# State space tables and phases on VectorE, parameters of both layers at once, and finer pieces stepped by VectorE's load

## The chip, the cores and the metric

The kernel runs on one core of a Trainium2 chip. Its engines work side by side, each from a queue of its own, and wait for one another by semaphores: TensorE (PE, with its weight loads PEld), VectorE (DVE), ScalarE (ACT), GpSimd (POOL) and SyncE (SP), which here issues DMAs. The metric is the time of one execution on the device in microseconds (us), as the median of the runs.

## What is computed

Two layers of a backbone over 1024 latent tokens and 256 context tokens of width 1024, in float32. In each layer a normed and modulated input is projected once, and three groups of heads share the columns: six latent attention heads, a bidirectional state space part (S5) of 16 groups with 16 channels and 64 states, and six windowed attention heads. Their outputs are joined, projected and added; then a gated MLP with a small convolution follows. Cut to what matters here:

```python
def s5_discretize(a_re, a_im, log_dt, b_re, b_im):
    lam = lax.complex(a_re, a_im)
    dt = jnp.exp(log_dt)[:, None]
    a_bar = jnp.exp(lam * dt)
    b_bar = ((a_bar - 1.0) / lam)[:, :, None] * b_mat
...
for l in range(DEPTH):
    cq, ckv, kr, u, qs, ks, vs = jnp.split(h @ w_in[l], IN_OFFSETS, axis=-1)
    ya = mla_latent_attention(...)     # six heads, softmax over all tokens
    yb = s5_bidirectional(u, ...)      # h[t] = a_bar h[t-1] + b_bar u[t], both directions, y = Re(C h) + D u
    yc = swa_latent_attention(...)     # windowed heads
    x = x + g1 * (jnp.concatenate([ya, yb, yc], axis=-1) @ w_out[l])
    x = x + g2 * conv_ffn(rms_norm(x, norm2[l]) * (1.0 + sc2) + sh2, ...)
```

## The kernel before

Each layer runs through an input projection, an attention stage, an output projection and the MLP. The change is in the attention stage, from about 296 to 723 us in layer 0 and from 2107 to 2500 us in layer 1.

**The latent heads** set the stage's pace. A unit is one head and one chunk of tokens (512, 512 or 256). `mla_prep` makes it ready: it transposes kn and qn on PE, splits them into a rounded part (kh, qh, by ACT) and a rest (kl, ql, by DVE, line 98), and then takes the maximum of the scores: twelve products b<-kh,qh on PE, each followed by a `tensor_reduce` to mx on DVE (line 1336), then nm (line 1340), which a transposition, ACT and a DMA carry into a row of qh. `mla_steps` then runs the unit's ten steps (two for the short chunk): three products into s on PE, an exponential to p on ACT, one product av on PE. The preparation of the next unit is drawn in between the steps of this one.

**S5** runs as a side job in the same stage. It is a Python generator, `s5()`; wherever it yields, a piece ends. `side.share(done, nsteps * 5 // 6)` after each attention step draws as many pieces as bring it level with its share, in layer 0 all pieces by step 110 of 132. `S5N` gives the number of pieces, 161 and 138. The work goes by quarters of four groups, with the 128 partitions holding two directions of 64 states, and time cut into 160 windows of eight tokens:
- parameters: from a_re, a_im and log_dt, by some 170 DVE instructions on 16 to 64 columns, the powers pw of a_bar, the decay rho, the factor of bb, and a ladder ec, ei of squarings of the rotation of one step;
- `windows`: the channels transposed into windows, with copies cpx and cpl on DVE (lines 1049, 1050);
- `tables(k)`: output map cv and input map q of quarter k, complex products of pc or pq (powers in window order) with C or bb; six products of 128x640 and six of 128x512, all on GpSimd;
- `phases(k)`: the rotations E of 160 windows, by doubling from one column, eight levels of six products each, all on GpSimd;
- `maps(k)`: q transposed to wl, and cv x bb multiplied on PE to the map inside a window (strip, Mt); `inputs(k)`: ug x wl on PE; `recur(k)`: rotate by E, scan with rho (line 1156), rotate back to Sg, on DVE; `outputs(k)`: Mt x ug and cv x Sg on PE; `back`: channels back to rows.

A third job, `mods`, sums later layers' modulation vectors on DVE (macc<-mw,srow,macc, line 98), drawn in the same way. PE's matmuls of preparation, S5 and mods share three PSUM banks b; the scores s have three of their own.

The order in which each engine gets its instructions is not the program's order: a list scheduler places them, so that work of several jobs is mixed. Each engine then runs its own list strictly in order. Loads go through SP's queue in the same fixed way. All the helpers `mul`, `add` and `sub` record line 80, `ts` lines 93 and 95, `stt` line 98, `act` line 77, `mm` line 65 and `tr` line 74, so rows are told apart by their tiles. In the changed kernel all DVE instructions carry line 50.

Of the kernel before, what the change touches and what calls it, by code (L numbers as in the profile page):

```python
# [8 lines left out]
F32 = mybir.dt.float32  # L9
F32R = mybir.dt.float32r  # L10
I32 = mybir.dt.int32
# [21 lines left out]
def trunk(ctx, tc, x, c, ctxt, c_ctx, w_mod, b_mod, norm1, w_in, q_lora_g, w_uq, kv_lora_g, w_ukv,  # L33
# [4 lines left out]
    V, S, G, PE = nc.vector, nc.scalar, nc.gpsimd, nc.tensor  # L38
# [65 lines left out]
    def load_split(hi, lo, raw, srcs, scale=None):  # L104
        """DRAM pieces into raw, then hi = the rounded value and lo = what is left of it."""
        for dst, src in srcs:
            nc.sync.dma_start(out=dst, in_=src)
        if scale is None:
            act(hi, raw)
            sub(lo, raw, f32(hi))  # L110
        else:
            act(hi, raw, AF.Copy, scale=scale)
            stt(lo, raw, scale, f32(hi), ALU.mult, ALU.subtract)

    class Wsets:
        """Rotating sets of (rounded, rest, raw) weight tiles over the pools that are open."""
# [49 lines left out]

    def k8(t):
        return t.rearrange("p (k n) -> p k n", k=8)
# [72 lines left out]
    def mod_cols(psf, pl, acc, l, nm, k0, n, nj):  # L241
        """Sums over the partitions of acc, n blocks of 128 columns for each of nj."""
# [13 lines left out]
    def mod_gen(l, nm, nj, pl, psf, w):  # L256
        """One modulation vector, with the sums over the rows on the vector engine."""
# [15 lines left out]
    def norm_stats(big, sm, psf, xs, ci, rn, o=0, n=None, eng=None):  # L273
        """rn[p, i] = 1 / rms of token i * 128 + p of the chunk (or of n of its tokens from o)."""
# [22 lines left out]
    def norm_apply(tb, rbt, psf, rn, xs, at, A, sh, ci, o=0, n=None, eng=G):  # L297
        """at = x * rn * A + sh, split; tb and rbt are scratch."""
# [24 lines left out]
    def load_mov(cols, src, k0, m):  # L323
        """Columns of rows k0.. as a moving operand: m tiles of 128 rows in one set."""
# [27 lines left out]
    def s1_tiles(t0, m):  # L352
        """Tiles of tokens side by side, as the rows of the operands arrive."""
# [87 lines left out]
    def params(rows, name):  # L441
        """Vectors of both layers, rows of 128 values each, with the channel on the partitions."""
# [71 lines left out]

    for l in range(2):
# [6 lines left out]
        # ======== input projection ========  # L522
# [45 lines left out]
        def rope_table(g, half):  # L568
            """Cosines and sines of the latent tokens, times the gains of the dimensions they meet."""
# [9 lines left out]
        def rope(xv, tab, g, t, nh, half, eng=None):  # L579
            """Gain and rotation of [128, 2, nh, 2 half] in place, two tiles of tokens."""  # L580
# [35 lines left out]
        # k_rope, windowed keys and values, with the token on the partitions  # L616
# [51 lines left out]
        def s3(state):  # L668
            """Keys and values of the latent attention, from a chunk of c_kv."""
# [35 lines left out]
        def s5q(state):  # L705
            """Queries of the latent attention, from a chunk of c_q."""
# [25 lines left out]
        def s7(t0):  # L732
            """Queries of the windowed attention."""
# [108 lines left out]
        # ======== S5 ========  # L842
        def s5():
            sp = s5p
            cnt = [0]
# [10 lines left out]
            def s16(dt=F32, n=16):  # L856
                cnt[0] += 1
                return sp.tile([128, n], dt, name=f"s16_{cnt[0]}")

            prm = sp.tile([128, 3, 16], F32, name="prm")  # L860
            ld = sp.tile([16, 2], F32, name="ld")
            nc.sync.dma_start(out=ld, in_=log_dt[l].rearrange("d g -> g d"))
            ps = bank([128, 512])
            for i, src in enumerate((a_re, a_im, None)):
                st = sp.tile([16, 2, 64], F32, name=f"pst{i}")
                if src is None:
                    V.tensor_copy(st, ld.unsqueeze(2).to_broadcast([16, 2, 64]))
                else:
                    nc.sync.dma_start(out=st, in_=src[l].rearrange("d g p -> g d p"))
                tr(ps[:, i * 16:(i + 1) * 16], st.rearrange("g d p -> g (d p)"))  # L870
            V.tensor_copy(prm.rearrange("p a g -> p (a g)"), ps[:, 0:48])
            lre, lim = prm[:, 0, :], prm[:, 1, :]

            def expo(dst, xin):
                xc, k, r, q = s16(), s16(), s16(), s16()
                ki, kj = s16(I32), s16(I32)
                ts(xc, xin, -87.0, 88.0, ALU.max, ALU.min)
                ts(k, xc, 1.4426950408889634, MAGIC)
                ts(k, k, -MAGIC, op0=ALU.add)
                stt(r, k, -0.693359375, xc)  # L880
                stt(r, k, 2.12194440e-4, r)
                ts(q, r, 1.0 / 5040)
                for cf in (1.0 / 720, 1.0 / 120, 1.0 / 24, 1.0 / 6, 0.5, 1.0):
                    stt(q, q, cf, r, ALU.add, ALU.mult)
                ts(q, q, 1.0, op0=ALU.add)
                ts(ki, k, 127.0, op0=ALU.add)
                ts(kj, ki, 23, op0=ALU.logical_shift_left)
                mul(dst, q, kj.bitcast(F32))

            def sincos(co, si, a):  # L890
                k, r, z, p, s0, c0 = (s16() for _ in range(6))
                ki, k1 = s16(I32), s16(I32)
                m, sg, w = s16(), s16(), s16()
                ts(k, a, 0.6366197723675814, MAGIC)
                ts(k, k, -MAGIC, op0=ALU.add)
                stt(r, k, -1.5703125, a)
                stt(r, k, -4.837512969970703125e-4, r)
                stt(r, k, -7.549789948768648e-8, r)
                mul(z, r, r)
                ts(p, z, -2.5052108385441720e-8, 2.7557319223985893e-6)  # L900
                mul(p, p, z)
                for cf in (-1.9841269841269841e-4, 8.3333333333333333e-3, -1.6666666666666667e-1):
                    stt(p, p, cf, z, ALU.add, ALU.mult)
                mul(p, p, r)
                add(s0, p, r)
                ts(p, z, 2.0876756987868099e-9, -2.7557319223985888e-7)
                mul(p, p, z)
                for cf in (2.4801587301587302e-5, -1.3888888888888889e-3, 4.1666666666666667e-2, -0.5):
                    stt(p, p, cf, z, ALU.add, ALU.mult)
                ts(c0, p, 1.0, op0=ALU.add)  # L910
                V.tensor_copy(ki, k)
                ts(k1, ki, 1, op0=ALU.bitwise_and)
                V.tensor_copy(m, k1)
                ts(w, m, -1.0, 1.0)
                mul(r, s0, w)
                mul(z, c0, m)
                add(si, r, z)
                mul(r, c0, w)
                mul(z, s0, m)
                add(co, r, z)  # L920
# [46 lines left out]
            for _ in range(10):  # L967
                nr, ni = s16(), s16()
                if _ == 5:
                    yield  # L970
# [1106 lines left out]
```

## Time and profile before

| | us |
|---|---|
| median of three runs | 3424.99 |
| lowest, highest run | 3420.28, 3428.63 |
| the profiled execution's span | 3426.8 |
| PE busy in it | 3253.7 (95%) |
| DVE busy | 2339.9 (68%) |
| ACT busy | 1167.5 (34%) |
| POOL busy | 486.9 (14%) |

A row of a timeline tells when an instruction started and how long the profiler had it in its engine, with the time that the engine sat idle ahead of it and what released it in brackets. "Busy" thus includes time in which an instruction has started and makes no headway. Windows give the busy time of each engine in a stretch, and the TensorE clock that was granted, as a share of full speed (1.00 is 2.4 GHz, 0.50 is 1.2 GHz).

### The profile page before, as it was taken

The numbers are of one execution on the slowest core, as the hardware profiler recorded it, in microseconds if no ns is written. First come the engines' busy times: TensorE is split into PE (matmuls) and PEld (weight loads), VectorE is DVE, ScalarE is ACT, GpSimd is POOL, SyncE is SP. The second block draws the span as 40 slices with busy tenths as digits, with TensorE's granted clock in tenths as the row PEclk, the third lists the DMA queues.
The fourth block names the chain that finished last, engine by engine and source line by source line (L and its number), as shares of the span: only waits on it lengthen the run. The fifth ranks groups of instructions, "written<-read, shape, count | busy, mean of one in ns | idle before, by whom it ended". The sixth has DMA issues, their size and how long they took to land. (4 is left out here: it accounts for less than half of the span.)

```text
span 3426.8 us, 43150 instructions
## 1 busy us (share of the span) xinstructions
PE 3253.7 (95%) x15950; PEld 2597.1 (76%) x15950; DVE 2339.9 (68%) x4391; ACT 1167.5 (34%) x2076; POOL 486.9 (14%) x787
## 2 busy tenths in 40 slices
PE   8999769999999999999999999679999999999999
PEld 5897446667888888888888887446677788888888
DVE  7778786885687766667666768776762665555655
ACT  3532225555152222222223442234563422222221
POOL 2332561000020000000000432471000100000000
PEclk9999789999999999999999999789999999999999
DMA  7434111333512222222212344010324111111211
GB/s 247 132 87 125 32 50 41 98 116 100 166 47 77 64 73 73 64 65 78 62 59 68 101 117 116 18 31 23 87 71 124 44 44 49 56 43 43 62 37 56
DMA packets 401325, 260.84 MB, mean 76 GB/s; under 512 B 173647, under 2 KB 370393, under 8 KB 401113
## 3 DMA queue, kind: packets, MB, share of 16 engines
q1 hardware_dynamic: 400466, 257.80, 26.0%
q8 instruction: 126, 2.06, 0.2%
q14 instruction: 86, 0.70, 0.1%
q10 hardware_dynamic: 647, 0.26, 0.0%
HBM read 206.22 MB, written 49.46 MB: 75 GB/s over the span
## 5 line engine op out<-in xcount | busy, mean ns | idle before, releaser
L65 PE MATMUL u<-ah,wh 128*128 128x512 f32 (+1 forms) x1760 | 649.9, 370 | 2.3 <-ACT ah L77 1.6
L65 PE MATMUL u<-al,wh 128*128 128x512 f32 (+1 forms) x1760 | 648.9, 369 | 1.4 <-POOL al L80 1.1
L65 PE MATMUL u<-ah,wl 128*128 128x512 f32 (+1 forms) x1760 | 648.3, 368 | 0.0
L77 ACT ACTIVATE wh<-raw 128x1024 fp32r<-128x1024 f32 (+3 forms) x184 | 189.2, 1038 | 720.5 <-PE d L65 292.2
L98 DVE SCALAR_TENSOR_TENSOR cv<-u,par,cv 128x511 f32<-128x511 f32 (+2 forms) x616 | 326.1, 555 | 135.6 <-ACT cv L77 130.4
L65 PEld LDWEIGHTS u<-al,wh 128*128 128x128 f32 x1760 | 332.3, 189 | 58.2 <-POOL al L80 2.2
L65 PEld LDWEIGHTS u<-ah,wh 128*128 128x128 f32 x1760 | 332.0, 189 | 57.8 <-ACT ah L77 1.8
L65 PEld LDWEIGHTS u<-ah,wl 128*128 128x128 f32 x1760 | 332.2, 189 | 55.3
L80 DVE TENSOR_TENSOR wl<-raw,wh 128x1024 fp32r<-128x1024 f32 (+3 forms) x184 | 220.1, 1200 | 160.0 <-ACT wh L77 158.9
L98 DVE SCALAR_TENSOR_TENSOR x<-d,g,x 128x512 f32<-128x512 f32 (+2 forms) x307 | 209.5, 685 | 108.8 <-PE d L65 108.6
L98 DVE SCALAR_TENSOR_TENSOR macc<-mw,srow,macc 128x256 f32<-128x256 f32 (+1 forms) x364 | 231.3, 660 | 67.1 <-DMA mw<-in_w_mod_dram 65.8
L77 ACT ACTIVATE cv<-u,par,par 128x512 f32<-128x512 f32 (+1 forms) x220 | 159.7, 728 | 323.1 <-PE u L65 320.9
L65 PE MATMUL av<-p,v 128*65 128x512 f32 (+1 forms) x504 | 260.7, 601 | 0.0
L77 ACT ACTIVATE p<-s 128x512 f32<-128x512 f32 (+1 forms) x252 | 147.6, 586 | 236.4 <-PE s L65 233.1
L65 PE MATMUL d<-ah,wh 128*128 128x512 f32 (+2 forms) x614 | 224.8, 366 | 1.8 <-DVE x L98 1.6
L65 PE MATMUL d<-al,wh 128*128 128x512 f32 (+2 forms) x614 | 223.5, 364 | 0.0
L65 PE MATMUL d<-ah,wl 128*128 128x512 f32 (+2 forms) x614 | 223.4, 364 | 0.0
L1336 DVE TENSOR_REDUCE mx<-b 128x1 f32<-128x512 f32 (+1 forms) x300 | 165.6, 586 | 47.6 <-PE b L65 46.3
L65 PE MATMUL b<-kh,qh 96*128 96x512 f32 (+1 forms) x300 | 124.7, 462 | 63.0 <-DVE ql L98 46.0
L65 PE MATMUL s<-qh,kh 97*128 97x512 f32 (+1 forms) x252 | 154.0, 611 | 0.0
L65 PEld LDWEIGHTS b<-kh,qh 96*128 96x128 f32 x300 | 57.9, 199 | 114.5 <-DVE ql L98 50.8
L65 PE MATMUL av<-sp,sv 128*65 128x384 f32 x320 | 129.0, 492 | 6.5 <-ACT sden L77 3.4
(373 smaller groups left out, 6689.4 us busy)
## 6 DMA issues: line engine op xcount, KB each, us to landing
raw<-in_w_up_dram SPq DMA_DIRECT2D x88, 512.0 KB
mw<-in_w_mod_dram SPq DMA_DIRECT2D x224, 128.0 KB
raw<-in_w_down_dram SPq DMA_DIRECT2D x44, 512.0 KB
mw<-in_w_mod_dram SPq DMA_DIRECT2D x48, 256.0 KB
wm<-in_w_mod_dram SPq DMA_DIRECT2D x16, 512.0 KB
xd<-x SPq DMA_DIRECT2D x32, 256.0 KB
raw<-in_w_in_dram SPq DMA_DIRECT2D x14, 512.0 KB
sqd<-sqb SPq DMA_DIRECT2D x36, 192.0 KB
```

Source lines behind the costliest of these rows:

```text
L65: PE.matmul(out, lhsT, rhs, start=start, stop=stop)
L77: S.activation(out, in_, func, **kw)
L80: (eng or V).tensor_tensor(out, a, b, op=op)
L98: V.scalar_tensor_tensor(out, a, s, b, op0=op0, op1=op1)
L1336: V.tensor_reduce(mx[:, j, i:i + 1], ps[:, :w], axis=AX.X, op=ALU.max)
```

## The change

Five things are altered together.

1. `tables(k)` runs on VectorE, the input map q first and then cv; every product is followed by a yield. GpSimd keeps only the memsets of Sg in this stage.
2. `phases(k)` is no longer a doubling. E is one complex outer product of two small tables, EP (10 values, coarse) and EQ (16 values, fine): six products of 128x640 per quarter, on VectorE.
3. The parameters of both layers are worked out together, once, by `s5_params` in layer 0's stretch where the u features are projected, on tiles with a layer axis. They go to DRAM (pmd, 128x1168 values for each layer, 598 KB) and `s5()` reads its layer's part back into pm with one DMA. Layer 1 works out none.
4. The copies cpx, cpl, pc, pq and the negated nct move from VectorE to ScalarE.
5. The pieces are finer, and a piece weighs what it costs: `Metered` wraps VectorE and adds 100 plus the elements of each instruction to a load; `Weighed.to` advances by 200 plus the load that a piece recorded. `S5N` becomes 175700 and 166800. `phases(k)` moves behind `inputs(k)`, `tables(k + 1)` behind `recur(k)`.

```diff
-    V, S, G, PE = nc.vector, nc.scalar, nc.gpsimd, nc.tensor
+    S, G, PE = nc.scalar, nc.gpsimd, nc.tensor
+    class Metered:
...
+            def call(out, *args, **kw):
+                self.load += 100 + max(int(np.prod(a.shape[1:])) for a in (out, *args[:1]) if hasattr(a, "shape"))
+                return fn(out, *args, **kw)
+            return call
+    V = Metered(nc.vector)
...
-    S5N = [161, 138]
+    S5N = [175700, 166800]
...
+    class Weighed(Side):
+        def to(self, k):
+            while self.k < k and not self.done:
+                at = V.load
+                try:
+                    next(self.g)
+                except StopIteration:
+                    self.done = True
+                self.k += 200 + V.load - at
...
+    def s5_params(sp, psf):
...
+        for l in range(2):
+            ld = sp.tile([16, 2], F32, name=f"ld{l}")
+            nc.sync.dma_start(out=ld, in_=log_dt[l].rearrange("d g -> g d"))
...
+        V.tensor_copy(prm.rearrange("p a l g -> p (a l g)"), ps[:, 0:96])
+        yield
...
+        for E, lev, size in ((EQ, 3, 16), (EP, 7, 10)):
...
+                cmul(E[0][:, :, n:n + m, :], E[1][:, :, n:n + m, :], E[0][:, :, 0:m, :], E[1][:, :, 0:m, :], er, ei2, sh)
+                n *= 2
+                lev += 1
+                yield
+        for l in range(2):
+            nc.sync.dma_start(out=pmd[l], in_=J[:, l, :])
+        yield
...
+            pm = sp.tile([128, NPRM], F32, name="pm")
+            nc.sync.dma_start(out=pm, in_=pmd[l])
+            pw, rho, (fr, fi), EP, EQ = prm_views(pm)
...
-                V.tensor_copy(pc[i][0:64, 0:9, :], pw[i][0:64])
+                act(pc[i][0:64, 0:9, :], pw[i][0:64])
...
-            ts(nct, ct[1], -1.0)
+            act(nct, ct[1], AF.Copy, scale=-1.0)
...
-                        V.tensor_copy(cpx, unc[:, :, cs])
-                        V.tensor_copy(cpl, un[:, :, cs])
+                        act(cpx, unc[:, :, cs])
+                        act(cpl, un[:, :, cs])
...
-                mul(t1, pr, cr, G)
-                mul(t2, pi, ci_, G)
-                sub(cv[0], t1, t2, G)
+                mul(t1, pr, cr)
+                yield
+                mul(t2, pi, ci_)
+                yield
+                sub(cv[0], t1, t2)
+                yield
...
-                n, lev = 1, 3
-                while n < 160:
-                    m = min(n, 160 - n)
...
+                a = [z[:, :, gs].rearrange("p t g -> p g t").unsqueeze(3).to_broadcast(sh) for z in EP]
+                b = [z[:, :, gs].rearrange("p t g -> p g t").unsqueeze(2).to_broadcast(sh) for z in EQ]
+                Ev = [z.rearrange("p g (a b) -> p g a b", a=10) for z in E]
+                yield from cmul(Ev[0], Ev[1], a[0], a[1], b[0], b[1], sh, "pm")
...
-            tables(0)
+            yield from tables(0)
             yield from windows(0)
-            phases(0)
             for k in range(4):
                 yield from maps(k)
-                if k < 3:
-                    tables(k + 1)
                 if k == 2:
                     yield from windows(1)
                 yield from inputs(k)
+                yield from phases(k)
                 yield from recur(k)
                 if k < 3:
-                    phases(k + 1)
+                    yield from tables(k + 1)
                 yield from outputs(k)
...
-        side = Side(s5(), S5N[l])
+        side = Weighed(s5(), S5N[l])
+        if l == 0:
+            prm_pool, close_prm = open_pool("prm", side=sd)
+            prms = Side(s5_params(prm_pool, lambda: cps.tile([128, 512], F32, tag="b", name="b", bufs=3)), 30)
+            prms.to(1)
...
-                if f * 3 + ci == 2:
-                    side.to(6)
+                if l == 0:
+                    prms.share(f * 3 + ci + 1, 6)
         prep.finish()
+        if l == 0:
+            prms.finish()
+            close_prm()
+        side.to(1)
```

How it stands on three engines, all in layer 0. First GpSimd, where the phases of quarter 1 end and the tables of quarter 2 begin (E: phases; pm, cm: halves of complex products), before:

```order
L80 TENSOR_TENSOR E_4459<-cm_4533,cm_4534 128x4x32
L80 TENSOR_TENSOR E_4460<-cm_4535,cm_4536 128x4x32
L80 TENSOR_TENSOR pm_4752<-pc_3808,ct_3780 128x640
L80 TENSOR_TENSOR pm_4753<-pc_3809,ct_3781 128x640
L80 TENSOR_TENSOR pm_4754<-pc_3808,nct 128x640
L80 TENSOR_TENSOR pm_4755<-pc_3809,ct_3780 128x640
L80 TENSOR_TENSOR cv_4748<-pm_4752,pm_4753 128x640
L80 TENSOR_TENSOR cv_4749<-pm_4754,pm_4755 128x640
```

and the changed kernel's whole GpSimd work at S5's start in layer 0:

```order
L1368 MEMSET v_0_3095 128x10
L1368 MEMSET v_1_3099 128x10
L1248 MEMSET Sg_4368 64x4
L1249 MEMSET Sg_4368 64x4
L1248 MEMSET Sg_4369 64x4
L1249 MEMSET Sg_4369 64x4
L1248 MEMSET Sg_4894 64x4
L1249 MEMSET Sg_4894 64x4
```

Of 717 rows on GpSimd 221 are left, and in this stage only memsets.

Second VectorE, where the first tables become due. Before, the last copies of parameters are followed by mods' macc and by ql and mx of head 0's short chunk (96x256):

```order
L1018 COPY pq_3811<-pw_3385 64x128
L1019 COPY pq_3811<-pw_3385 64x128
L93 TENSOR_SCALAR nct<-ct_3781 128x256
L98 SCALAR_TENSOR_TENSOR macc<-mw,srow,macc 128x512 x2
L98 SCALAR_TENSOR_TENSOR ql<-b,gcol,qh 96x256
L1336 TENSOR_REDUCE mx<-b 128x1 x2
L98 SCALAR_TENSOR_TENSOR macc<-mw,srow,macc 128x512
L1340 TENSOR_REDUCE nm<-mx 128x2
L98 SCALAR_TENSOR_TENSOR macc<-mw,srow,macc 128x512
```

and after, from the last parameters (prmJ) on; pm is the tile read back from DRAM, cm<-pq,bb the first of the tables:

```order
L50 TENSOR_TENSOR pt_3754<-prmJ,s_54_3606 128x64
L50 TENSOR_TENSOR prmJ<-pt_3753,pt_3754 128x2x32
L50 TENSOR_TENSOR cm_3835<-pm,bn_3811 128x256
L50 TENSOR_TENSOR cm_3836<-pm,bn_3812 128x256
L50 TENSOR_TENSOR cm_3837<-pm,bn_3812 128x256
L50 TENSOR_TENSOR bb_3813<-cm_3835,cm_3836 128x256
L50 TENSOR_SCALAR macc<-mw,srow 128x512 x2
L50 TENSOR_TENSOR cm_3838<-pm,bn_3811 128x256
L50 TENSOR_TENSOR cm_3888<-pq_3868,bb_3813 128x512
L50 TENSOR_TENSOR bb_3814<-cm_3837,cm_3838 128x256
L50 TENSOR_TENSOR cm_3891<-pq_3869,bb_3813 128x512
```

The reading of pm and the tables now stand here, on the engine that also makes mx; the short chunk's ql and mx stand ahead of these rows, among the parameters.

Third TensorE, at the maps of quarter 0 (q transposed, then cv x bb), before:

```order
L65 MATMUL av<-p,v_0_3093 65x512
L74 MATMUL b<-ident,q_3828 128x128 x4
L65 MATMUL b<-kh_3099,qh 128x512 x2
L65 MATMUL s<-qh,kh_3095 128x512
L65 MATMUL s<-ql,kh_3095 128x512
L65 MATMUL b<-kh_3099,qh 128x256
L65 MATMUL s<-qh,kl 128x512
L74 MATMUL b<-ident,q_3829 128x128 x4
L65 MATMUL av<-p,v_0_3093 65x512
L65 MATMUL b<-kh_3099,qh 128x512
L65 MATMUL b<-cv_3826,bb_3776 16x128
```

and after:

```order
L80 MATMUL s<-qh,kl 128x256
L80 MATMUL av<-p,v_0_3095 65x512
L80 MATMUL av<-p,v_0_3095 65x256 x2
L89 MATMUL b<-ident,q_3886 128x128 x4
L89 MATMUL b<-ident,q_3887 128x128 x4
L80 MATMUL b<-cv_3884,bb_3813 16x128
L89 MATMUL b<-ident,kn 96x128 x8
L80 MATMUL b<-cv_3885,bb_3814 16x128
L80 MATMUL b<-cv_3884,bb_3813 16x128
```

Before, score steps of the first head (s, av) and the next head's b<-kh,qh stand among the maps; now the maps follow the first head's last av, and the transposes of kn for the second head stand among them.

## Rows read from the trace of the kernel before

**Rows 1.** The page's first part: engine, busy us, share of the span, instructions.

```profile
PE 3253.7 (95%) x15950; PEld 2597.1 (76%) x15950; DVE 2339.9 (68%) x4391; ACT 1167.5 (34%) x2076; POOL 486.9 (14%) x787
```

**Rows 2.** Slices of 86 us: length, busy of each engine, granted clock, DMA share, GB/s.

```profile
342.00:428.00 86.00, 62.52 (x252) 37.82 (x252) 65.26 (x81) 22.97 (x49) 49.36 (x109) 0.74 0.13 34
428.00:514.00 86.00, 57.27 (x288) 37.74 (x286) 73.34 (x76) 25.04 (x52) 54.18 (x90) 0.82 0.18 50
2141.00:2227.00 86.00, 58.55 (x216) 35.16 (x217) 62.81 (x82) 25.02 (x50) 43.53 (x76) 0.72 0.08 18
2227.00:2313.00 86.00, 61.60 (x293) 39.83 (x292) 67.42 (x70) 26.57 (x53) 61.44 (x128) 0.85 0.12 31
```

**Rows 3.** Short windows of layer 0, same columns.

```profile
308.70:362.70 54.00, 46.20 (x173) 26.73 (x171) 50.91 (x201) 20.77 (x39) 30.92 (x55) 0.87 0.38 97
310.00:320.00 10.00, 10.00 (x38) 6.12 (x37) 10.00 (x55) 3.78 (x7) 0.00 (x0) 1.00 0.89 201
490.00:500.00 10.00, 0.00 (x0) 0.00 (x0) 10.00 (x1) 0.00 (x0) 10.00 (x9) 0.50 0.00 0
620.00:630.00 10.00, 9.81 (x43) 6.51 (x41) 9.33 (x17) 7.36 (x15) 0.00 (x0) 1.00 0.52 133
```

**Rows 4.** PE's waits, 296 to 600 us: line, releaser, us in total, times, longest.

```profile
PE b L65 <- DVE ql L98: 28.8, 3, 21.0
PE b L74 <- DVE mx L1336: 18.1, 1, 18.1
PE b L74 <- DVE cpx L1049: 3.5, 1, 3.5
```

**Rows 5.** PE's waits, 2107 to 2320 us, same columns.

```profile
PE b L65 <- DVE mx L1336: 23.7, 3, 13.9
PE b L65 <- DVE ql L98: 16.9, 1, 16.9
PE b L74 <- DVE mx L1336: 4.5, 1, 4.5
```

**Rows 6.** Timeline of DVE: start us, us, line, operation, out<-in, count [idle before].

```profile
360.76 19.23 DVE L98 SCALAR_TENSOR_TENSOR macc<-mw,srow,macc 128x512 f32<-128x512 f32 x1
...
439.93 9.31 DVE L80 TENSOR_TENSOR t<-E,sv 128x640 f32<-128x640 f32 x1
...
480.12 22.46 DVE L98 SCALAR_TENSOR_TENSOR macc<-mw,srow,macc 128x512 f32<-128x512 f32 x2
...
2162.93 20.31 DVE L1049 COPY cpx<-unc 32x128 f32<-32x128 f32 x1 [3.35 <-PE b L74]
...
2248.90 10.66 DVE L80 TENSOR_TENSOR t<-E,sv 128x640 f32<-128x640 f32 x1 [1.42 <-ACT sv L77]
...
2287.23 19.09 DVE L80 TENSOR_TENSOR num<-num,den 128x1024 f32<-128x1024 f32 x1
```

**Rows 7.** Timeline of POOL, layer 0, the row at 378.18.

```profile
378.18 1.26 POOL L80 TENSOR_TENSOR q<-cm,cm 128x512 f32<-128x512 f32 x1
```

**Rows 8.** Attention stages of layers 0 and 1 whole, columns of rows 2.

```profile
296.00:723.00 427.00, 367.22 (x1668) 235.03 (x1667) 348.70 (x722) 172.21 (x352) 130.40 (x266) 0.91 0.26 69
2107.00:2500.00 393.00, 338.67 (x1457) 214.21 (x1456) 285.53 (x595) 160.16 (x316) 122.30 (x266) 0.90 0.19 48
```

**Rows 9.** Timeline of DVE, layer 0, three products of 128x640 in a row.

```profile
413.79 2.28 DVE L80 TENSOR_TENSOR u<-E,sv 128x640 f32<-128x640 f32 x3
```

**Rows 10.** The page's fifth part, mx: busy us, mean ns | idle before, releaser.

```profile
L1336 DVE TENSOR_REDUCE mx<-b 128x1 f32<-128x512 f32 (+1 forms) x300 | 165.6, 586 | 47.6 <-PE b L65 46.3
```

**Rows 11.** Timeline of layer 0's start: SP's queue, PE, DVE, PE.

```profile
293.16 0.43 SPq L869 DMA_DIRECT2D pst<-in_s_a_im_dram  x1
...
308.70 0.39 PE L65 MATMUL s<-qh,kh 97*128 97x512 f32 x1
...
313.61 0.34 DVE L80 TENSOR_TENSOR s<-s,s 128x16 f32<-128x16 f32 x3
...
380.74 1.09 PE L74 MATMUL b<-ident,q 128*128 128x128 f32 x4 [18.05 <-DVE mx L1336]
```

More of the change, by code (lines that the diff above doesn't have):

```diff
@@ L37, in trunk, with __init__, __getattr__ @@
     nc = tc.nc
-    V, S, G, PE = nc.vector, nc.scalar, nc.gpsimd, nc.tensor
+    S, G, PE = nc.scalar, nc.gpsimd, nc.tensor
+    class Metered:
+        def __init__(self, eng):
+            self.eng, self.load = eng, 0
+        def __getattr__(self, name):
+            fn = getattr(self.eng, name)
+            def call(out, *args, **kw):
[3 more added lines that the diff above has]
+    V = Metered(nc.vector)
     dbg = dbg or {}
@@ L513, in trunk, with prm_views @@
     applied = ()
+    NPRM = 2 * 144 + 16 + 32 + 2 * 160 + 2 * 256
+    pmd = [dram.tile([128, NPRM], F32, name=f"pmd{l}") for l in range(2)]
+    def prm_views(t):
+        o, r = 0, []
+        for shape in ((9, 16), (9, 16), (16,), (16,), (16,), (10, 16), (10, 16), (16, 16), (16, 16)):
+            n = int(np.prod(shape))
+            v = t[..., o:o + n]
+            if len(shape) == 2:
+                v = (v.rearrange("p (n g) -> p n g", g=16) if len(t.shape) == 2 else
+                     v.rearrange("p l (n g) -> p l n g", g=16))
+            r.append(v)
+            o += n
+        return r[0:2], r[2], r[3:5], r[5:7], r[7:9]
@@ L844, in s5 @@
             sp = s5p
-            cnt = [0]
             def bank(shape):
@@ L854, in bank @@
                 return v
[L856 to L888, printed above, removed]
@@ L961, in s5, with cmul @@
-            yield
-            rho, e2 = s16(), s16()
-            mul(e2, mag, mag)
-            mul(rho, e2, e2)
-            mul(rho, rho, rho)
-            ec, ei = [co], [si]
[L967 to L970, printed above, removed]
-                cmul(nr, ni, ec[-1], ei[-1], ec[-1], ei[-1], [128, 16], "tm")
-                ec.append(nr)
-                ei.append(ni)
+            def cmul(orr, oi, ar, ai, br, bi, shape, tag):
+                t1, t2, t3, t4 = (sp.tile(shape, F32, tag=f"{tag}{i}", name=f"cm{i}") for i in range(4))
+                mul(t1, ar, br)
+                mul(t2, ai, bi)
+                yield
+                sub(orr, t1, t2)
+                mul(t3, ar, bi)
+                yield
+                mul(t4, ai, br)
+                add(oi, t3, t4)
+                yield
@@ L1060, in tables @@
                 q = [sp.tile([128, GQ, 8, 16], F32, tag=f"q{i}", name=f"q{i}") for i in range(2)]
+                sh = [128, GQ, 8, 16]
+                pr, pi = (pq[i][:, :, gs].rearrange("p t g -> p g t").unsqueeze(3).to_broadcast(sh) for i in range(2))
+                br, bi = (bb[i][:, gs, :].unsqueeze(2).to_broadcast(sh) for i in range(2))
+                yield from cmul(q[0], q[1], pr, pi, br, bi, sh, "pm")
                 sh = [128, GQ, 10, 16]
@@ L1064, in tables @@
                 t1, t2, t3, t4 = (sp.tile(sh, F32, tag=f"pm{i}", name=f"pm{i}") for i in range(4))
-                mul(t1, pr, cr, G)
-                mul(t2, pi, ci_, G)
-                sub(cv[0], t1, t2, G)
-                mul(t3, pr, nci, G)
-                mul(t4, pi, cr, G)
-                sub(cv[1], t3, t4, G)
-                sh = [128, GQ, 8, 16]
-                pr, pi = (pq[i][:, :, gs].rearrange("p t g -> p g t").unsqueeze(3).to_broadcast(sh) for i in range(2))
-                br, bi = (bb[i][:, gs, :].unsqueeze(2).to_broadcast(sh) for i in range(2))
-                cmul(q[0], q[1], pr, pi, br, bi, sh, "pm", G)
+                mul(t1, pr, cr)
+                yield
+                mul(t2, pi, ci_)
+                yield
+                sub(cv[0], t1, t2)
+                yield
+                mul(t3, pr, nci)
+                yield
+                mul(t4, pi, cr)
+                yield
+                sub(cv[1], t3, t4)
+                yield
                 st8["cv", k], st8["q", k] = cv, q
```

249 lines of the change are left out of this document (149 added, 100 removed).

## Prediction

> **What bounds the kernel now.** I read the page's first part, then the span in stretches, then what PE waits for, then the engine it waits for. PE is busy 3253.7 of 3426.8 us [rows 1]: PE is the bound, and only stretches in which it idles or runs slow can give anything. Those are two, one in each layer, where the state space part runs beside the latent heads. Four slices of 86 us show it: PE busy 62.52, 57.27, 58.55 and 61.60 us, together 104.1 us of 344 idle, at granted clocks of 0.74 to 0.85, which means part of the time at the lower level (1.2 GHz) [rows 2]. Look at these slices inside [rows 3]: from 490 to 500 PE and ACT do nothing, and DVE and POOL are both "busy" for all 10 us; DVE's ten are one single instruction, and the clock is at 0.50. From 620 to 630 POOL is silent, and PE does 9.81 us beside 9.33 us of DVE at full clock.
>
> PE's waits name DVE: in layer 0 28.8 us for ql, 18.1 for mx and 3.5 for the copies cpx [rows 4]; in layer 1 23.7, 16.9 and 4.5 for mx and ql [rows 5]. DVE, in turn, is held inside an instruction: macc takes 19.23 us, a product of 128x640 9.31, a pair of macc 22.46, then in layer 1 a copy of 32x128 20.31, again a product of 128x640 10.66, and one of 128x1024 19.09 [rows 6]. Neither macc nor the copy reads a POOL result. What they share is the end: POOL's row of q<-cm,cm starts at 378.18 and takes 1.26, so POOL stops at 379.44, and the macc ends at 379.99 [rows 6, 7]. So POOL's tables and phases hold DVE, DVE's mx and ql come late, and PE has nothing to score.
>
> The Trainium skill, "SBUF — State Buffer", section "Who interferes with whom", says that a VectorE instruction with two SBUF inputs, or a copy in a mode that takes both ports, and a GpSimd one that reads SBUF exclude each other, the second blocked until the first ends. The trace agrees on who is held and differs on how long: 19.23 us outlast the 1.26 us of one POOL instruction many times over. By the page six holds would be some 8 us and their removal worth as little; by the rows they are 101 us.
>
> **What the change takes away.** All of this POOL work goes, 130.4 us of POOL in layer 0's stage and 122.3 in layer 1's [rows 8]; only memsets stay on POOL there.
> - Waits: layer 0's 28.8 + 18.1 + 3.5 = 50 us (cpx moves to ACT), layer 1's 23.7 + 16.9 + 4.5 = 45 [rows 4, 5].
> - Clock: layer 0's two slices lack (0.26 + 0.18) x 86 = 37.8 us of full clock, layer 1's (0.28 + 0.15) x 86 = 37.0 [rows 2]. If all 52 us of their idle time were at 0.50, 26 of it would lie in idle time and 11 to 12 in work. If none were, all 37. The 10-us row has 0.50 in an idle stretch [rows 3], but a long wait begins at full clock, so I take 18 in each, bounds 11 and 37.
>
> So 50 + 18 = 68 us in layer 0 and 45 + 18 = 63 in layer 1: 131 in all, if nothing new came.
>
> **What it adds.**
> - *Tables and phases on DVE.* Per layer four quarters of 12 products of 128x640 (6 of tables, 6 of phases) and 6 of 128x512. Three u<-E,sv of 128x640 take 2.28 us, 0.76 each [rows 9]; by width 128x512 is then 0.61. 48 x 0.76 + 24 x 0.61 = 51 us a layer. Removed from DVE: 32 copies cpx and cpl, by width some 0.15 each, 5 us, and as much for pc, pq and nct, 10 us. DVE's stage in layer 0 has 348.7 us of 427; its three holds are 51 us [rows 6] where some 3 would do, so 300 without them. With 51 added, 10 off and 5 more for parameters (below) it has 346. PE has 367 less the 18 of slow clock, 349. They are level. Layer 1: 285.5, less 48 for its three, plus 51, less 10 and 15, is 264, against PE's 339 less 18, 321 [rows 8]. So DVE stays under PE in layer 1 and beside it in layer 0.
> - What is late next in layer 0 is therefore DVE. It can be full while PE is full: 310 to 320 has both at 10.00 us [rows 3]. But at a head's boundary PE waits for twelve mx in a row, and now tables stand among them. I take 8 us for layer 0, bounds 0 and 30.
> - *Copies to ACT.* ACT works 172 of 427 us [rows 8]; 32 copies more lie in its idle time; where one comes ahead of an exponential the step waits for one short copy. I take nothing, bounds 0 and 5 us a layer.
> - *Parameters of both layers.* After the order, 219 small instructions stand between the first copies and the first bb, with 26 mx and 9 others among them. Three 128x16 products take 0.34 us, so 0.085 each behind the first [rows 11]; twice as wide they may be 0.1. 219 x 0.09 = 20, plus 35 x 0.59, an mx's mean [rows 10], 41 us on DVE. (Before there are 174 such, 15 us, for each layer, so layer 0 has 5 more and layer 1 15 less.) It can start when pst has landed. Its issue is at 293.16 today and hardly moves [rows 11]; so about 295 to 336. Head 0's first kl now stands behind that pst, and its first score, 308.70 today [rows 11], comes up to 5 us later; I take 3. SP passes six parameter loads ahead of ud and kn; these are in those 3 us.
> - *The trip through DRAM.* In the order, DVE's next instruction behind the last parameter reads pm, so DVE itself waits for two writes and one read of 598 KB; queued behind are macc, the tables and head 1's kl. At the 201 GB/s of 310 to 320, with the DMA engines 0.89 busy [rows 3], one write and the read (1.2 MB) take 6 us and all three 9; at the stage's mean of 69 GB/s [rows 8] all three take 26. Bounds 6 and 26; I take 10, since the fast row is that of this very stretch. Then bb (eight of 128x256, by width 0.3 each), the 12 products of tables (8 us) and four macc (0.6 each): 13 us, and cv is ready near 359.
> - *Who waits for it.* PE has head 0's 22 steps meanwhile. It began them at 308.70 and met its 18.05 us wait at 362.7 with a few steps left [rows 11]; of these 54 us it was busy 46.2 [rows 3]. With 3 us of later start, and the last steps against the slow clock in it, they reach to about 358. So the trip is just hidden. But in the new order q, cv x bb, kn, ug x wl and twelve b all come with no score step between them. On DVE that chain is 3 kl, 4 products of phases, ql and 12 mx, 16 x 0.6 + 4 x 0.76 = 13 us, and nm's way through a transposition, ACT and a DMA to qh, for which I have no row; it lies between nothing and the 9 us of the big trip, I take 4. Of these 17 us PE's own short matmuls fill between nothing and half; I take 12 idle, and 3 for a trip that is longer: 15, bounds 5 (the scores reach further) and 35 (a trip of 26).
> - Clock after that idle stretch: layer 0 has half its slow work back, 6 us, bounds 0 and 15.
> - Layer 1 has no parameters to wait for, its pm is read early; its first tables (8 us) come before head 1's mx. 12 us with clock, bounds 3 and 30.
> - *Finer pieces by load.* They only place the same work; nothing is priced for them but the bounds above.
>
> Sum: layer 0 68 - (3 + 15 + 8 + 6) = 36; layer 1 63 - 12 = 51. 87 us off 3426.8 is 3340; the profiled run's span stands 1.8 us over the median, so 3338.
>
> **The rivals.**
> - *A, DVE becomes layer 0's bound.* For: 346 against 349 us, and the slice 428 to 514 was 73.34 of 86 busy, 0.85, holds included [rows 2]. At 0.85 the stage takes 346 / 0.85 = 407 us and layer 0 gains 20; at 0.82, today's share [rows 8], 5. With layer 1's 51: 3354 to 3369, with its bound of 33 up to 3387. Against: 620 to 630 with 9.33. The Trainium skill, "Perfetto Trace Analysis", section "Optimizing Scalar/DVE Operations", advises moving work off a saturated VectorE, and so speaks against this change; it adds that moving it to GpSimd might not help, since they share a port, and rows 6 bear the addition out.
> - *B, nearly all comes back.* The order hides the trip and the chain at the head's boundary as it hid 310 to 320: costs of 5 in layer 0 and 3 in layer 1, so 131 - 8 = 123: 3302.
> - *C, slower.* The maps of every quarter become a boundary like layer 0's first, where q, cv x bb and twelve mx follow each other with no score step. There are eight quarters; idle time and slow clock of 16.4 us at each (8 x 16.4 = 131) eat the whole gain, and at 20 it ends at 3425 + 160 - 131 = 3454. It decides from 16.4 on; I have 15 + 6 at layer 0's first and 2 to 4 at the others. For: maps and mx share the three b banks. Against: at the later quarters the order keeps one to three score steps among the maps.
> - *D, DVE was not held by POOL.* Then some 41 us a layer are added to DVE and the holds stay: within 0.2% or slower. Against: the ends agree within 0.6 us [rows 6, 7].
>
> **How the numbers follow.** Forecast 3338 with 0.55, own range 3312 to 3356. A 0.20, B 0.13, C 0.08, D 0.04. Faster by over 0.2% (7 us, about what this measurement tells from no change) are the forecast, A and B: 0.88. D's middle gives 0.04 for the same, C 0.08 for slower. The range 3295 to 3390 takes in B and A with both ends of the trip, and leaves out C and D.
>
> **What would show it.** Right: no DVE instruction of a 128x640 or smaller over 3 us in either stage; the four slices at PE 75 or more and clock near 0.95; POOL nearly empty there. The trip: a DVE wait of 8 to 13 us for a DMA of pm in layer 0, PE idle 10 to 20 us near 360 to 385. A: PE waits for mx and kl, a few us at each of layer 0's boundaries, DVE over 90% busy from 340 to 560. C: the same in both layers at 17 us each. Wrong altogether, if holds of 10 us stay with POOL silent.

## The result, and the profile after

The changed kernel takes 3345.19 us (median of four runs, 3342.85 to 3352.68) against 3426.2 for the kernel before on the same occasions: a ratio of 0.9768, 95% interval 0.9754 to 0.9783. It is 81 us faster; 3338 was forecast, and the range was 3295 to 3390.

First the page's first part of the kernel after, which answers to [rows 1], and the slices that answer to [rows 2], layer 1's shifted by the 33 us by which it now begins earlier:

```profile
PE 3240.7 (97%) x15950; PEld 2596.9 (78%) x15950; DVE 2315.2 (69%) x4324; ACT 1190.7 (36%) x2166; POOL 237.4 (7%) x291
...
342.00:428.00 86.00, 64.31 (x216) 38.77 (x216) 73.72 (x150) 30.97 (x71) 0.40 (x4) 0.74 0.23 68
428.00:514.00 86.00, 82.84 (x444) 55.60 (x443) 80.58 (x129) 41.58 (x93) 0.40 (x4) 0.98 0.26 72
2108.00:2194.00 86.00, 77.57 (x345) 50.26 (x346) 74.81 (x117) 42.38 (x96) 0.40 (x4) 0.84 0.11 26
2194.00:2280.00 86.00, 84.80 (x370) 52.11 (x368) 73.06 (x125) 42.91 (x91) 0.79 (x8) 1.00 0.15 39
```

Three of the four bad slices are mended in busy time; the first of layer 0 is not: PE 64.31 of 86 (62.52 before), clock 0.74 as before. Layer 1's first slice has its clock at 0.84 still. The stages whole, which answer to [rows 8]:

```profile
296.00:692.00 396.00, 363.67 (x1668) 236.78 (x1667) 352.07 (x796) 185.17 (x400) 1.76 (x18) 0.93 0.29 80
2074.00:2419.00 345.00, 331.73 (x1468) 213.83 (x1467) 260.02 (x453) 172.97 (x362) 1.75 (x18) 0.96 0.21 55
```

Layer 0's stage went from 427 to 396 us, layer 1's from 393 to 345. PE's last latent score of layer 0 starts at 689.49 instead of 720.68, so layer 0 gave 31 us. From its first to its last score layer 1 took 365.8 us before and takes 317.4, so it gave 48, and 2 more came ahead of its first score. In the DVE rows of the kernel after no instruction (mx and the like aside) that took over 1.9 us overlaps any work of POOL from 296 us on; before there were six, of 100 us in all.

What is left in layer 0 stands in DVE's timeline (start us, us, operation, out<-in [idle before]; its first row is the factor of bb, ready long before the last parameter), in PE's (same columns), and in five windows:

```profile
321.88 0.19 DVE L50 TENSOR_TENSOR prmJ<-prmJ,s 128x32 f32<-128x32 f32 x1
...
351.95 0.23 DVE L50 TENSOR_TENSOR prmJ<-pt,pt 128x64 f32<-128x64 f32 x1
358.86 1.10 DVE L50 TENSOR_TENSOR cm<-pm,bn 128x256 f32<-128x256 f32 x3 [6.68 <-DMA mw<-in_w_mod_dram]
...
364.08 1.28 DVE L50 TENSOR_TENSOR q<-cm,cm 128x512 f32<-128x512 f32 x2
```

```profile
357.82 1.08 PE L80 MATMUL av<-p,v 128*65 128x256 f32 x4 [1.62 <-ACT den L92]
364.91 1.94 PE L89 MATMUL b<-ident,q 128*128 128x128 f32 x8 [6.00 <-DVE q L50]
369.77 0.58 PE L80 MATMUL b<-cv,bb 64*16 64x128 f32 x2 [2.93 <-DVE cv L50]
...
395.42 0.37 PE L89 MATMUL b<-ident,nm 128*4 128x128 f32 x1 [2.39 <-DVE nm L50]
```

```profile
350.00:360.00 10.00, 7.29 (x26) 3.52 (x24) 3.12 (x14) 5.81 (x14) 0.00 (x0) 0.97 0.64 233
360.00:370.00 10.00, 2.17 (x10) 1.70 (x10) 10.00 (x18) 3.78 (x12) 0.00 (x0) 0.50 0.33 86
370.00:380.00 10.00, 10.00 (x44) 6.37 (x43) 7.66 (x10) 2.94 (x5) 0.00 (x0) 0.50 0.28 75
380.00:390.00 10.00, 7.69 (x30) 5.48 (x28) 8.77 (x15) 4.26 (x14) 0.00 (x0) 0.84 0.26 62
390.00:400.00 10.00, 5.44 (x14) 3.58 (x15) 10.00 (x19) 0.95 (x2) 0.12 (x2) 0.51 0.16 46
```

The last parameter is written at 352. DVE then stands still for 6.68 us; the bracket names a load of mw, but the instruction reads pm, and the window beside it shows the DMA engines at 233 GB/s (0.64 busy): it is the trip through DRAM. Head 0's scores end at 356 and q is ready at 365. From then until nm at 395 PE has S5's maps and the preparation of the second head, but no score step, and its clock is 0.50 from 360 to 380, 0.84 and 0.51 in the two windows after.

### The profile page after: what moved, and what is told of

Same layout as the page of the kernel before. It is cut to its first block, busy times and chain, and to the rows that moved or that the text cites. A ratio compares the mean times of both kernels' runs of the same rounds, so it can differ in the third digit from the quotient of the medians.

```text
span 3344.2 us, 42621 instructions
## 1 busy us (share of the span) xinstructions
PE 3240.7 (97%) x15950; PEld 2596.9 (78%) x15950; DVE 2315.2 (69%) x4324; ACT 1190.7 (36%) x2166; POOL 237.4 (7%) x291
## 5 line engine op out<-in xcount | busy, mean ns | idle before, releaser
L80 PE MATMUL av<-p,v 128*65 128x512 f32 (+1 forms) x504 | 253.1, 585 | 1.6 <-ACT den L92 1.6
L50 DVE SCALAR_TENSOR_TENSOR macc<-mw,srow,macc 128x256 f32<-128x256 f32 (+1 forms) x364 | 186.9, 539 | 65.9 <-DMA mw<-in_w_mod_dram 65.4
L50 DVE SCALAR_TENSOR_TENSOR x<-dx,g,x 128x512 f32<-128x512 f32 (+2 forms) x141 | 97.3, 690 | 51.4 <-PE dx L80 51.3
```

The lines of the kernel that those rows point to most:

```text
L50: return fn(out, *args, **kw)
L80: PE.matmul(out, lhsT, rhs, start=start, stop=stop)
```

## The experiments

Each kernel ran beside the kernel before on one chip. Ratios are to that; the changed kernel's is 0.977.

| kernel | median us | ratio, 95% interval |
|---|---|---|
| changed | 3345.2 | 0.9754 to 0.9783 |
| tables back on GpSimd | 3397.3 | 0.9896 to 0.9930 |
| phases back on GpSimd | 3360.9 | 0.9788 to 0.9819 |
| both back on GpSimd | 3390.4 | 0.9870 to 0.9903 |
| pieces by number | 3346.9 | 0.9748 to 0.9777 |
| kernel before, engine alone | 3342.3 | 0.9733 to 0.9768 |
| copies back on VectorE | 3355.1 | 0.9767 to 0.9815 |
| without the trip | 3335.0 | 0.9713 to 0.9748 |
| without the parameters' arithmetic | 3314.3 | 0.9649 to 0.9689 |
| engine and copies in the kernel before | 3338.3 | 0.9725 to 0.9758 |
| each layer's own parameters | 3329.0 | 0.9696 to 0.9729 |
| loads first, without the trip | 3328.0 | 0.9695 to 0.9725 |
| own parameters, loads first | 3330.3 | 0.9698 to 0.9724 |

### Is it the engine? Back on GpSimd, in the changed kernel

In `tables` or `phases` or both, each product goes to GpSimd and still counts for the weight of its piece:

```diff
-                mul(t1, pr, cr)
+                gp(mul, t1, pr, cr)
```

Tables: 

> The changed kernel with the 12 products of tables(k) back on GpSimd, as pieces of the same weight; all else as changed (3345 us). Theory H1 (GpSimd's run of products holds VectorE's two-input instructions): each quarter's run is 6 x 1.4 + 6 x 1.15, about 15 us, and a product, a macc or an Sg of VectorE that comes into it shows 5 to 15 us; PE idles behind it; 3370 to 3400. Rival H2 (the gain came from finer pieces placed by load): placement is unchanged and VectorE has 33 us less a layer, so 3330 to 3350 and no VectorE instruction over 3 us.

Phases: 

> The changed kernel with the six products of the outer product in phases(k) back on GpSimd. H1: runs of six products, 6 x 1.4 = 8 us, so holds of up to 8 us, at most eight of them; 3350 to 3375. H2: 3330 to 3350, no VectorE instruction over 3 us.

Both: 

> The changed kernel with tables and phases both on GpSimd: the engine alone undone, while the outer product, the finer pieces, the parameters of both layers and the copies on ScalarE stay. H1: most of the gain is gone, 3385 to 3420, six or more holds of 8 us or longer. H2: 3325 to 3350. If the copies on ScalarE were the gain (H3): 3345 within 5 us.

Measured: 3397.3, 3360.9 and 3390.4 us. All three times fall where H1 said, none where H2 or H3 put it. But the long holds that H1 was to show are few. With the tables on GpSimd no instruction of DVE's that overlaps POOL takes over 2.6 us (5 to 15 were expected), with the phases there none over 2.3 (up to 8). DVE and POOL mostly take turns; first DVE's timeline, then POOL's:

```profile
374.36 4.86 DVE L50 TENSOR_TENSOR cm<-pm 128x640 f32<-128x640 f32 x2 [5.28 <-POOL cv L95]
```

```profile
372.80 1.52 POOL L95 TENSOR_TENSOR cv<-pm,pm 128x640 f32<-128x640 f32 x1
374.29 1.33 POOL L95 TENSOR_TENSOR pm<-pc,ct 128x640 f32<-128x640 f32 x1
375.69 2.43 POOL L95 TENSOR_TENSOR cv<-pm,pm 128x640 f32<-128x640 f32 x1
...
382.93 4.38 POOL L95 TENSOR_TENSOR q<-cm,cm 128x512 f32<-128x512 f32 x1
```

Two DVE products take 4.86 us, twice what they take alone; POOL's cv takes 2.43 instead of 1.5. POOL can be held as well: its q takes 4.38 us instead of 1.26 [rows 7], while three of DVE's two-input instructions run. The longest waits behind POOL here are of another kind: DVE waits for POOL to give back the scratch tiles that tables and phases share, and PE waits for q and cv. These waits arise from splitting the two functions, so this run doesn't price the holds. DVE's and PE's in layer 0 of that kernel (releaser, us in total, times, longest):

```profile
DVE cm L50 <- POOL cv L95: 26.6, 3, 13.5
```

```profile
PE b L89 <- POOL q L95: 10.7, 2, 10.2
...
PE b L80 <- POOL cv L95: 6.4, 2, 4.7
```

Only with both on GpSimd do long holds come back, one in each layer, of 8.46 and 7.73 us; six or more of 8 us were expected. DVE's row of the first, then POOL's at the same time:

```profile
458.66 8.46 DVE L50 TENSOR_TENSOR t<-E,sv 128x640 f32<-128x640 f32 x1 [2.25 <-POOL pm L95]
```

```profile
458.51 1.68 POOL L95 TENSOR_TENSOR cm<-pm 128x640 f32<-128x640 f32 x1
460.13 1.56 POOL L95 TENSOR_TENSOR cv<-pm,pm 128x640 f32<-128x640 f32 x1
461.63 4.82 POOL L95 TENSOR_TENSOR cm<-pm 128x640 f32<-128x640 f32 x3
```

The t is held for all five and goes on when POOL's last one ends, at 466.45. But a run of products without a wait of POOL's own is not enough for a hold. Earlier in this kernel POOL works from 364.75 to 416.96 without a pause, on 32 products and a memset, and 40 instructions of DVE lie in that stretch (busy us of PE, PEld, DVE, ACT and POOL, clock, DMA), the longest of them the macc below:

```profile
364.75:416.96 52.21, 28.05 (x97) 18.54 (x97) 41.88 (x40) 10.66 (x24) 52.21 (x33) 0.57 0.17 46
```

```profile
387.36 2.12 DVE L50 SCALAR_TENSOR_TENSOR macc<-mw,srow,macc 128x512 f32<-128x512 f32 x1
```

So H1 stands in that GpSimd is the cost, and falls in part of its mechanism: in the kernel before 22 products lay in the first hold and 28 in the third, but what else than an unbroken run makes a hold, and not turns, no run here shows. This kernel also shows how the other parts of the change act once the work stays on GpSimd: 39 us of gain remain.

### The engine alone

The kernel before with the two functions on VectorE, 12 products and 48 in one piece each:

```diff
-                mul(t1, pr, cr, G)
+                mul(t1, pr, cr)
...
-                    cmul(E[0][:, :, n:n + m], E[1][:, :, n:n + m], E[0][:, :, 0:m], E[1][:, :, 0:m], er, ei2, s2, "pm", G)
+                    cmul(E[0][:, :, n:n + m], E[1][:, :, n:n + m], E[0][:, :, 0:m], E[1][:, :, 0:m], er, ei2, s2, "pm")
```

> The kernel before (3429 us beside these runs) with tables(k) and phases(k) on VectorE and nothing else altered: still coarse pieces stepped by number, phases by doubling, parameters in each layer, copies on VectorE. H1 (the holds by GpSimd's unbroken runs of 20 to 28 products are the cost): no VectorE instruction over 3 us, 60 to 80 us less than before, 3350 to 3370. H2' (VectorE can take the work only in finer pieces): tables are one piece of 12 products, 8 us, and phases one of 48, 7 us, ahead of mx; at fourteen places PE waits 4 to 8 us for them, 3385 to 3420.

Measured: 3342.3 us, 8 below H1's span and 43 below H2's. No instruction of VectorE takes over 1.5 us in the two stages. The engine alone gives the whole gain, as far as the intervals tell the two apart. But not in the same place: here layer 0's last score starts at 675.4, 14 us earlier than in the changed kernel, and layer 1 takes 322.4 us from first to last score, 5 more. Another 5 us lie between the two layers' attention stages; that stretch varies as much (1398.7 to 1404.2 us) among the changed kernels whose code is the same there, so they are not read as an effect. Layer 0's first slices:

```profile
296.00:342.00 46.00, 45.91 (x194) 29.65 (x192) 44.63 (x237) 17.21 (x32) 0.00 (x0) 1.00 0.44 110
342.00:428.00 86.00, 76.53 (x365) 50.83 (x366) 79.54 (x227) 36.50 (x80) 0.40 (x4) 0.90 0.20 51
428.00:514.00 86.00, 77.55 (x365) 49.39 (x363) 80.29 (x191) 35.21 (x73) 1.23 (x8) 0.94 0.23 61
```

PE does 76.53 us from 342 to 428 where the changed kernel does 64.31; in the next slice it is the other way round. So the rest of the change gives something from quarter 1 on and in layer 1, and takes more at layer 0's start.

### Finer pieces, and the copies

```diff
-    S5N = [175700, 166800]
+    S5N = [263, 240]
...
-        side = Weighed(s5(), S5N[l])
+        side = Side(s5(), S5N[l])
```

> The changed kernel with its finer pieces stepped by their number (263 and 240) instead of by VectorE's load. H1: the pieces only place the same work, 3335 to 3360. H2: 3370 or more, with VectorE overfull in some slices and PE waiting for mx there.

Measured: 3346.9 us, the same. The load as a weight does nothing that the number of fine pieces does not. Neither the fine pieces themselves nor the outer product in the phases were undone alone, so what each is worth stays open.

```diff
-                        act(cpx, unc[:, :, cs])
-                        act(cpl, un[:, :, cs])
+                        nc.vector.tensor_copy(cpx, unc[:, :, cs])
+                        nc.vector.tensor_copy(cpl, un[:, :, cs])
```

(and pc, pq and nct likewise.) 

> The changed kernel (3345 us) with cpx, cpl, pc, pq and nct back on VectorE. If VectorE is not the bound: 3340 to 3352. If the copies on ScalarE were a part of the gain of their own (H3): 3355 or more, about 10 us of VectorE in each layer.

Measured: 3355.1 us, 10 more and at the edge of H3's case, though the intervals overlap (0.9767 to 0.9815 against 0.9754 to 0.9783). It isn't VectorE's price of 10 us in each layer: layer 0's last score comes 6 us later, and layer 1 takes 317.5 us from first to last score, as in the changed kernel. In the other direction, added to the engine alone in the kernel before:

> The kernel before with tables and phases on VectorE (3342 us) and, besides, the copies cpx, cpl, pc, pq and nct on ScalarE; pieces, phases by doubling and parameters of each layer as before. If the copies give the 10 us that their undoing cost in the changed kernel: 3328 to 3335, and a kernel better than the changed one. If that gain hung on the changed kernel's order: 3339 to 3345.

Measured: 3338.3 us, 4 less than the engine alone with intervals that overlap. So it falls between the two cases, nearer the second; that the gain of the copies hangs on the changed kernel's order is likely and not shown.

### What is lost at layer 0's start

```diff
+            if l == 0:
+                pm = prmJ[:, 0, :]
...
-        for l in range(2):
-            nc.sync.dma_start(out=pmd[l], in_=J[:, l, :])
+        nc.sync.dma_start(out=pmd[1], in_=J[:, 1, :])
```

> The changed kernel with layer 0 reading its parameters from the tile where they were computed, so without the trip through DRAM; layer 1 reads from DRAM as before. VectorE waits 6.7 us for the trip, and PE waits for q behind it. If the trip is on the path: 5 to 10 us less, 3335 to 3340. If the long chain of parameters alone decides and the trip is hidden: within 2 us of 3345.

Measured: 3335.0 us, 10 less. The trace shows more than 6.68 us saved. DVE's row of the first q, which stands at 364.08 in the changed kernel:

```profile
331.84 0.68 DVE L50 TENSOR_TENSOR q<-cm,cm 128x512 f32<-128x512 f32 x1
```

Two of its windows, to be read against 43.43 and 64.31 us of PE in the changed kernel:

```profile
296.00:342.00 46.00, 37.54 (x153) 24.71 (x152) 42.22 (x202) 14.41 (x34) 0.00 (x0) 0.92 0.48 117
342.00:428.00 86.00, 73.24 (x348) 47.27 (x348) 79.56 (x180) 38.76 (x89) 0.40 (x4) 0.88 0.16 45
```

q is 32 us earlier, though the last parameters, the tables EP and EQ for the phases, now come as late as 376. The trip was a barrier: the DMA of layer 0's part had to wait for the last of 219 instructions, which work on both layers at once, before the first product of bb could have its factor. That factor was written at 322.1 in the changed kernel, after half of them, and first read at 358.9. Only 10 of the 32 us show in the time: the tables now stand among head 0's maxima on VectorE, and PE does 6 us less from 296 to 342.

The parameters' arithmetic left out:

```diff
-        lre, lim = prm[:, 0], prm[:, 1]
...
+        V.memset(J.rearrange('p l n -> p (l n)'), 0.5)
```

> The changed kernel without the arithmetic of the parameters: the tables of parameters are filled with one constant and still go through DRAM; all that follows runs as before. VectorE loses 219 small instructions ahead of layer 0's first tables. If their chain (to 352 us) is what keeps PE idle from 356 to 372 and slow behind it: 20 to 30 us less, 3315 to 3325. If the boundary itself (maps without score steps) is the cost: 8 us less at most, 3337 or more.

Measured: 3314.3 us, 31 less, just past the first case, and all of it in layer 0 (its last score at 657.0). The slice 342 to 428 is nearly whole:

```profile
342.00:428.00 86.00, 81.15 (x400) 52.15 (x400) 78.78 (x134) 42.68 (x99) 0.40 (x4) 0.98 0.19 47
```

So the parameters' arithmetic with its barrier is what layer 0's start still costs. Whether by the length of its chain or by the time that its 219 instructions take on VectorE, this run doesn't separate: it leaves out both. The boundary with no score step between the maps costs 5 us of idle time here at most.

Two ways to shorten the chain, and both together:

```diff
-            prms = Side(s5_params(prm_pool, lambda: cps.tile(...)), 30)
+            prmJ = s5p.tile([128, 1, NPRM], F32, name="prmJ")
+            prms = Side(s5_params(prm_pool, lambda: cps.tile(...), prmJ, l), 30)
```

> The changed kernel with each layer's parameters worked out in its own layer by the same generator, on tiles of half the width, and read where they lie (no trip in either layer). P1 (the 219 dependent small instructions cost the same at half the width; doing both at once spares layer 1 its own): against 3335 without the trip, layer 0 the same within 3 us and layer 1 5 to 12 us longer, 3338 to 3347. P2 (the double width is what makes layer 0's chain long): layer 0 8 us shorter, 3325 to 3333.

Measured: 3329.0 us, 6 less than without the trip at double width, with intervals that overlap. The time is in P2's range, but each of the two has a part of it. Layer 0's last score comes at 664.2, 14 us earlier. Layer 1 takes 319.9 us, 2 more, and 6.5 more pass between the layers (1407.9 us; in the changed kernels above 1398.7 to 1404.2), about what P1 gave layer 1. Nor is layer 0's gain all due to the width: with half as many loads ahead of it the parameters also begin 9 us earlier, as DVE's rows of prm show, without the trip, with own parameters, and in the next two kernels:

```profile
298.20 0.25 DVE L50 COPY prm<-b 128x96 f32<-128x96 f32 x1
```

```profile
288.89 0.21 DVE L50 COPY prm<-b 128x48 f32<-128x48 f32 x1 [1.62 <-PE b L89]
```

```profile
289.31 0.26 DVE L50 COPY prm<-b 128x96 f32<-128x96 f32 x1 [3.40 <-PE b L89]
```

```profile
289.41 0.21 DVE L50 COPY prm<-b 128x48 f32<-128x48 f32 x1 [1.46 <-PE b L89]
```

Loads first (the call of `prms.to(1)` moved ahead of `prep.to(1)`, without the trip, both layers at once): 

> The changed kernel without layer 0's trip through DRAM, and with the loads of the parameters ahead of the first head's loads in SP's queue. If the time at which the chain of parameters begins is on the path: it begins 5 us earlier, 3328 to 3332. If the first head's kl and mx are: they come 3 us later, 3336 to 3342.

Measured: 3328.0 us, 7 less than without the trip alone, at the lower end of the first case, though the intervals overlap (0.9695 to 0.9725 against 0.9713 to 0.9748). The chain begins 9 us earlier, not 5, and layer 0's last score comes at 669.3: at nearly the same start, own parameters are worth some 5 us of layer 0, not 14. Both together: 

> The changed kernel with each layer's parameters in its own layer, read where they lie (3329 us), and their loads ahead of the first head's in SP's queue (which was worth 7 us at the joint parameters without the trip). If the two add up: 3320 to 3325. If layer 0's chain is no longer what PE waits for once it has one layer's width: 3327 to 3333.

Measured: 3330.3 us; they don't add up. The rows above offer a reason: with own parameters the chain had begun at 288.89 already, and the loads ahead bring it no earlier. These three beat both kernels, by 15 to 17 us and by 100; which of them is best the intervals don't tell.

## Why the prediction was right, point by point

- **The holds.** Right: they are gone, and the engine alone gives the gain. Of layer 0's waits 50 us were to end and 26 to come (15, 3 and 8); PE's idle time in the stage fell by 27.5 us (59.8 to 32.3, [rows 8] against the stage rows above). In layer 1 it fell from 54.3 to 13.3, 41 us where 45 less part of 12 was forecast. Of the signs, no VectorE instruction of 128x640 or smaller is over 3 us (the longest takes 1.27). PE's 75 us hold in three slices of four, a clock near 0.95 in two.
- **Clock.** Mis-sized in layer 0: 18 less 6 us were to come back. The lack of clock in the stage went from 0.09 x 427 = 38 to 0.07 x 396 = 28 us, and with less idle time in it the slow work fell by some 4 us only (31 us of gain less 27.5). PE was idle for 10.5 us from 350 to 370, and its clock stood at 0.50 from 360 to 380 again. In layer 1 the two make up 48 - 41 = 7 us, where 18 less part of the 12 was forecast; since the 12 were not split, which part was off can't be told there.
- **The trip.** The wait was 6.68 us, 10 forecast and 8 to 13 given as its sign. The step that failed is the chain ahead of it: 41 us on DVE from 295, measured 52.6 (from prm at 299.6 to 352.2). It began 4.6 us later than the issue of pst had me think, and of its length the small instructions took some 35 us instead of 20 (52.6 less 17.9 for the others among them). A sum here waits for the two products ahead of it and the next product for the sum, as DVE's timeline shows:

```profile
340.16 0.29 DVE L50 TENSOR_TENSOR pt<-prmJ,s 128x32 f32<-128x32 f32 x2
340.49 0.19 DVE L50 TENSOR_TENSOR prmJ<-pt,pt 128x32 f32<-128x32 f32 x1
340.71 0.29 DVE L50 TENSOR_TENSOR pt<-prmJ,s 128x32 f32<-128x32 f32 x2
```

From 340.16 to 340.71 three instructions, 0.18 us each, where I had 0.09 from a row whose products don't wait for one another [rows 11]. "Just hidden" was thus wrong by 6 us of waiting for q, and the mechanism was not named: that the DMA ties the first factor to the last table. PE's idle time at the boundary was forecast as 15 and is 17.4 us (windows 350 to 400: 2.7, 7.8, 0, 2.3 and 4.6). That these are near is luck: the waits for q and cv, forecast at 3, come to 8.9, and those for the second head's preparation, forecast at 12, to 6.8.
- **First score.** 3 us later forecast, measured 4.5 (313.21).
- **VectorE beside PE.** 346 us forecast in layer 0, measured 352; 264 and 260 in layer 1. Rival A failed on its efficiency: from 428 to 514 DVE is 0.94 busy and PE 0.96, as in the one row of 620 to 630. One price was off: tables and phases take 61.5 us of VectorE in layer 0, not 51. A product of 128x640 takes 0.81 us, not 0.76, one of 128x512 0.68, not 0.61, and the outer product's first four, cm<-pm, take 1.25 (the groups of DVE in layer 0's stage, mean ns last):

```profile
L50 DVE TENSOR_TENSOR cm<-pm 128x640 f32<-128x640 f32 x16 | 19.5, 1248 | 0.0
...
L50 DVE TENSOR_TENSOR pm<-pc,ct 128x640 f32<-128x640 f32 x12 | 9.8, 814 | 0.0
```

- **Copies at nothing, pieces at nothing.** The pieces' weight is worth nothing, as said. The copies may not be: up to 10 us in the changed kernel, 6 of them in layer 0. I had counted what they free on VectorE's busy time only; how that reaches PE was not traced.
- **Sum.** 36 + 51 forecast, 31 + 50 measured: 6 us of error, 5 of them in layer 0, where the costs forecast at 32 were about 37: too little for chain and clock, partly made up by less idle time than forecast.
- **Rivals B, C, D.** B's 3302 is not reached by any kernel that computes its parameters; without them 3314. C's boundaries cost nothing like 16 us each: PE's waits from 428 on are a few us. D fell with the engine alone.

## What to carry to other kernels

When an engine shows an instruction of 20 us that takes 0.7 elsewhere, look which neighbour worked without a pause through it and ended with it, and price the move from the stages, not from the busy shares: VectorE took on 61.5 us of work in layer 0 and PE gained. Parts of a change that ride along need a run of their own; here one move carried the gain. The shared parameters with their trip took back what the rest gave: with own parameters in their place the changed kernel takes 3329.0 us, the engine alone 3342.3. A DMA of a tile makes its first reader wait for the last writer. And when a variant is to test one property, see that it starts at the same time: own parameters changed the width of the chain and its start at once.

## What the runs showed of the hardware

- In six holds of the kernel before a VectorE instruction stood for 8 to 28 of GpSimd's products, 9.31 to 21.8 us, and ended 0.1 to 1.1 us after GpSimd's last one before a wait; with both functions back on GpSimd five products made 8.46 us. Such a run doesn't always hold: the two also took turns, 2.4 us for products of 1.25 with the tables alone on GpSimd, and 2.12 at most on VectorE from 364.75 to 416.96 with both there. GpSimd can be held too (4.38 us for 1.26). Why macc passed in 0.7 to 1.8 us between GpSimd's products from 334 to 357 and stood from 360.76 on was not settled.
- The Trainium skill, "SBUF — State Buffer", section "Who interferes with whom", has the second instruction wait for the one that was first. The turns of 2.4 us agree with that; the holds of 8.46 to 21.8 us do not, since the next GpSimd instructions went ahead of a VectorE instruction that was waiting.
- With 0.94 of VectorE busy PE can still be 0.96 busy (428 to 514).
- A product of 128x640 took 1.25 us where one operand's last 16 values are read with a stride of 16 (cm<-pm), against 0.81 where they lie side by side (pm<-pc,ct). In both the other operand is repeated over those 16. No run changed the stride alone.
